# Weight blocks of odd and even depth placed 128 bytes apart, the other way round in the low parts, in a decoder layer on one core

## The chip, the cores and the metric

The program runs on one core of a Trainium2 chip. The metric is the device time of one execution in microseconds (us), as the median of several runs of the same program. Times of single instructions are given in nanoseconds (ns).

## What is computed

One decoder layer over 16 learned and 1024 given tokens of width 1024, all in float32: a gated feed-forward block, a mixing block (stick-breaking attention beside RWKV-7 time mixing), a second gated feed-forward block, and a final norm. Nearly all the arithmetic is in the dense products with the weights:

```
h = h + 0.5 * swiglu(rms_norm(h), ffn1_w_gate, ffn1_w_up, ffn1_w_down)   # 1024 -> 2816 -> 1024
proj = rms_norm(h) @ w_in                                               # 1024 -> 3232 columns
h = h + concat(sb_out, rw_out) @ w_out                                  # 1024 -> 1024
h = h + 0.5 * swiglu(rms_norm(h), ffn2_w_gate, ffn2_w_up, ffn2_w_down)
out = rms_norm(h, final_norm)
```

## The kernel before, in words

**The dense products.** Each float32 operand is split into a high part and a low part in a reduced float32 format, and each product is made of three matmuls (`mm3`): high weights with high activations, high weights with low activations, low weights with high activations. Such a group of three is called a triple here. Every matmul loads its own 128x128 weight block into TensorE while the matmul before it streams its activations past the array; the activations are called the moving operand, 512 columns of it, or 256 to 272, per matmul. A product over a depth of 1024 runs through eight depth blocks k = 0 to 7, so 24 matmuls into one PSUM bank; a product of the down projection runs through the two or four activation tiles of a part.

**The weight tiles.** `loads` fetches a raw weight tile of 128x1024 by DMA; `splits` and `wsplit` turn it into a high tile `whi` (ScalarE copies it) and a low tile `wlo` (VectorE subtracts), two buffers of each, taken in turn (`wtiles`). A tile holds `nk` depth blocks of `nm` columns, one behind the other, so that a depth block starts 512 bytes (for nm = 128) or a multiple of that behind the one before. Each tile is 1056 columns long, 4224 bytes, which is 128 more than 4096, so that the second buffer starts 128 bytes off the first, counted modulo 256. In the built program `whi` starts at byte 26912 and 31136 of each partition, `wlo` at 35360 and 39584: modulo 256 that is 32 and 160, 32 and 160.

**The moving operands.** The normed activations `nh` and `nl` are eight rows of 544 columns, 2176 bytes, so that row k+1 starts 128 bytes off row k modulo 256 (byte 96 for even k, 224 for odd). The activations of the down projection, `ah` and `al`, lie in four buffers of the same 544 columns and alternate in the same way. The normed activations of the second half in the last block, `n2B`, have rows of 512 columns: they keep their place modulo 256 from row to row.

**Places.** The place of a matmul is said here as the start of its moving operand minus the start of a weight block, modulo 256 bytes. It is 64 or 192 throughout these products. In the kernel before the weight blocks of one tile all start at the same byte modulo 256 while the rows of the activations alternate, so that both parts have place 64 for one k, both have 192 for the next, and so on; the other buffer has it the other way round. With `n2B` the place is the same for all k of a tile.

**The order.** A planner in the kernel (class `Clock`) plays the engines against each other with modelled costs and writes out the order of instructions for each engine; TensorE's stream is the dense products (task `dense`), into which triples and short runs of the mixing block's small matmuls are put. The stages the change tells apart are: 0 the first feed-forward block for the first half of the tokens, with its projections; 1 the same block for the second half, its projections and `w_out`; 2 the second feed-forward block for the first half and `w_out` for the second; 3 the second feed-forward block for the second half. Stage 3 and stage 0 make some of their gate and up products by another scheme (`pair`, `quad`) with weight tiles `qh` and `ql` of their own, which the change does not touch.

Of the kernel before, what the change touches and what calls it, by code (L numbers as in the profile page):

```python
# [16 lines left out]
P = 128  # L17
D = 1024
KT = D // P
# [21 lines left out]
WOUT = ((0, 1, 2, 3, 4, 5, 6, 7, 2, 3, 4, 5), (0, 1, 2, 3, 4, 5, 6, 7))  # L41
QF = dict(ffn1=6, ffn2=4)
LINE = 16
NQ, NCC = 6, 6
ROW = 544
AHEAD = 0.1
# [432 lines left out]
class Ker:  # L479
    def __init__(self, tc, A, out):  # L480
        self.tc, self.A, self.out = tc, A, out
        self.clock, self.fast = Clock(), None
        self.wq, self.wr, self.cur, self.flags = [], [], (), {}
        self.nc = NC(tc.nc, self.clock)
        self.need = self.clock.need
        self.after = lambda *aps: self.clock.need(*aps, slack=False)
# [38 lines left out]
        self.clock.ahead = False  # L525
        return raw

    def wtiles(self, nk, nm, pool):

        o = LINE * (pool is self.wx)  # L530
        t = [pool.tile([P, 8 * P + 2 * LINE], F32R, tag=t, bufs=2, name=n) for t, n in (("wh", "whi"), ("wl", "wlo"))]
        return [x[:, o:o + nk * nm].rearrange("p (k c) -> p k c", c=nm) for x in t]

    def wsplit(self, raw, nk, nm, pool):
        self.clock.ahead = True
        self.nsplit = getattr(self, "nsplit", 0) + 1
        hi, lo = self.wtiles(nk, nm, pool)

        self.split(hi, lo, raw, self.nc.gpsimd if self.nsplit < 3 else None)
        self.clock.ahead = False  # L540
        return hi, lo

    def loads(self, plan):

        for x in plan:
            if not isinstance(x, tuple):
                yield x
                continue
            raws = []
            if isinstance(x[0], tuple):  # L550
                for src, ring in zip(x[0], ((self.wp, "wr", 2), (self.fast.q, "wr2", 2))):
                    yield self.need(bank=ring)
                    raws.append(self.wraw(src, *x[1:3], ring))
                    self.hold(raws[-1:])
            else:
                yield self.need(bank=(self.wp, "wr", 2))
                raws.append(self.wraw(*x[:3]))
                self.hold(raws)
            self.wr.append((x, raws))
        self.wr.append(None)  # L560

    def splits(self):

        while True:
            yield lambda: self.wr
            if self.wr[0] is None:
                return
            x, raws = self.wr[0]
            if len(raws) == 2:
                self.wq.append((x, []))  # L570
                yield from self.pair(raws, self.wq[-1][1])
                self.drop(raws)
                self.wr.pop(0)
                continue
            raw, = raws
            pool = self.wx if len(x) > 3 else self.wp
            for tag in ("wh", "wl"):
                yield self.need(bank=(pool, tag, 2))
            self.wq.append((x, self.wsplit(raw, *x[1:3], pool)))
            self.hold(self.wq[-1][1])  # L580
            self.drop((raw,))
            self.wr.pop(0)
# [321 lines left out]
    def ffn(self, nm, h, n, chunks, edge, bank, first=None, hook=None, wx=False, poll=None, resid=None, done=None, wy=False, fast=False, once=False):  # L904
# [22 lines left out]
        def mm(wh, wl, name, c0, c1):  # L927
            yield self.need(*[x[k][:, c0:c1] for k in range(4) for x in n[0:2]], bank=self.nextbank)
            ps = bank(name)[:, :c1 - c0]
            for k in range(KT):  # L930
                if k == 4:
                    yield self.need(*[x[k][:, c0:c1] for k in range(4, KT) for x in n[0:2]])
                self.mm3(ps, wh[:, k, :], wl[:, k, :], nh[k][:, c0:c1], nl[k][:, c0:c1], k == 0, k == KT - 1)
                yield
            return ps

# [48 lines left out]
        def down(dh, dl, part, m, c0, c1):  # L985
            f0, f1 = part
            nf, mw, acts = f1 - f0, KT // (f1 - f0), act[f0:f1]
            yield self.need(acts[0][0][:, c0:c1], acts[0][1][:, c0:c1], bank=self.nextbank)
            pd = bank("pd")[:, :c1 - c0]
            ms = slice((m % mw) * P, (m % mw) * P + P)  # L990
            for j, (ah, al) in enumerate(acts):
                if j:
                    yield self.need(ah[:, c0:c1], al[:, c0:c1])
                self.mm3(pd, dh[:, j, ms], dl[:, j, ms], ah[:, c0:c1], al[:, c0:c1], j == 0, j == nf - 1)
# [218 lines left out]
    def proj(self, items, g, before=None, after=None):  # L1213


        nh, nl = self.n[0:2]
        ranges = ((0, 256), (256, 528)) if g == 0 else ((0, 256), (256, 512)) if len(items) > 1 else ((0, 512),)

        def load(col0, ncol):
            return self.wget(self.wcols("w_in")[:, :, col0:col0 + ncol], KT, ncol)  # L1220
        for i, (c0, c1) in enumerate(ranges):
            if before:
                yield from before(i)
            for col0, ncol, evac in items:
                if i == 0 or len(items) > 1:
                    wh, wl = yield from load(col0, ncol)
                yield self.need(*[x[k][:, c0:c1] for k in range(KT) for x in (nh, nl)], bank=self.nextbank)
                ps = self.bank("pd")[0:ncol, :c1 - c0]
                for k in range(KT):
                    self.mm3(ps, wh[:, k, :], wl[:, k, :], nh[k][:, c0:c1], nl[k][:, c0:c1], k == 0, k == KT - 1)  # L1230
# [52 lines left out]
    def plan(self):  # L1283
# [13 lines left out]
        def ffn(nm, poll=False, wx=False, fast=False, once=False):  # L1297
# [41 lines left out]
        yield from ffn("ffn1", wx=True, fast=True)  # L1339
        yield from proj(0)  # L1340
        yield from ffn("ffn1", once=True)
        yield from proj(1)
        yield from wout(False)
        yield from ffn("ffn2", True)
        if "woutat" not in F:
            yield lambda: F.get("f2b")
            F["woutat"] = None
            yield from wout(False)
        yield from ffn("ffn2", wx=True, fast=True)

    def projections(self, g, before, after):

# [667 lines left out]
    def wout(self, h2, n, hook, ready=None, late=False):  # L2020
# [5 lines left out]
        def one(m, wh, wl, i):  # L2026
# [3 lines left out]
            yield self.need(*[x[k][:, cs] for k in range(KT) for x in n[0:2]], bank=self.nextbank)  # L2030
            pd = self.bank("pwo")[:, 0:256]
            for k in range(KT):
                self.mm3(pd, wh[:, k, :], wl[:, k, :], n[0][k][:, cs], n[1][k][:, cs], k == 0, k == KT - 1)
                yield
            hd = h2[:, m, cs]
            with self.urgent():
# [504 lines left out]
```

## Time and profile before

| | |
|---|---|
| median of 3 runs | 2247.16 us (2245.82 to 2251.48) |
| profiled execution, its own time | 2247.88 us |
| its span, first to last instruction | 2246.0 us |
| TensorE matmul busy | 2218.6 us, 99% of the span |
| weight loads busy (beside the matmuls) | 1967.9 us, 88% |
| VectorE, ScalarE, GpSimd busy | 69%, 49%, 26% |
| granted TensorE clock, mean | 0.997 of full speed |

The recorded duration of a matmul reaches beyond the start of the next one, since matmuls are pipelined and their ends are modelled. What a matmul costs in a dense stretch is the step from its start to the next start; the differences in duration between neighbouring matmuls follow the differences in those steps.

### The profile page before, as it was taken

The page shows a single profiled execution, that of the slowest core. Times are in us where ns is not written, and L with a number is a line of the kernel's source. Part 1 is how long each engine was busy: PE and PEld are TensorE (multiplying, and loading weights), DVE is VectorE, ACT ScalarE, POOL GpSimd, SP SyncE. Part 2 cuts the span into 40 slices and gives each one's busy share as a digit, 9 for nine tenths or more (in the row PEclk, how much of TensorE's full clock was granted, in tenths as well). Part 3 has the DMA queues.
Part 4 walks back from the last instruction along what each step waited for, and adds up shares of the span by engine and source line. Part 5 has one row for each costly group of instructions (what it writes and reads, how often), then busy time and mean ns, then how long its engine had stood idle before and what let it go on. Part 6 is the DMA issues. An engine that isn't in the chain of part 4 may idle for free.

```text
span 2246.0 us, 41718 instructions
## 1 busy us (share of the span) xinstructions
PE 2218.6 (99%) x16409; PEld 1967.9 (88%) x16409; DVE 1547.6 (69%) x2633; ACT 1096.6 (49%) x2176; POOL 574.1 (26%) x722
## 2 busy tenths in 40 slices
PE   9999999999999999999999999999999999999998
PEld 8999999999878888778888988887878899899998
DVE  5887776476666655566576787556777656897774
ACT  5444444534444434655435564445656436455444
POOL 1321111013143231542012325314443101322120
PEclk9999999999999999999999999999999999999999
DMA  5543232545643232332556534334222433333332
GB/s 171 179 113 104 85 104 79 167 129 144 198 112 99 74 100 91 100 93 76 158 142 190 164 101 118 86 93 118 79 83 61 132 118 120 116 104 106 110 89 82
DMA packets 408730, 257.61 MB, mean 115 GB/s; under 512 B 45005, under 2 KB 392357, under 8 KB 408534
## 3 DMA queue, kind: packets, MB, share of 16 engines
q1 hardware_dynamic: 408534, 254.95, 39.3%
q8 instruction: 129, 2.11, 0.4%
q14 instruction: 67, 0.55, 0.1%
HBM read 220.90 MB, written 33.99 MB: 113 GB/s over the span
## 4 chain that ended last, share of the span: by engine, by line
PE 91%; DVE 3%; issue 2%; ACT 2%; DMA 1%; SPq 1%; POOL 0%; DVEq 0%; ACTq 0%; POOLq 0%
PE pd L107 33%; PE pu L107 21%; PE pg L107 21%; PE pwo L107 3%; PE px L107 3%; PE po L107 2%; PE pz L107 2%; PE pat L107 2%; DVE wlo L107 1%; SPq L107 1%; PE pG L107 1%; ACT whi L107 1%; PE psw L107 0%; PE pp L107 0%; DVE nl L107 0%
## 5 line engine op out<-in xcount | busy, mean ns | idle before, releaser
L107 ACT ACTIVATE whi<-wraw 128x1024 fp32r<-128x1024 f32 x314 | 330.7, 1053 | 324.7 <-PE pd L107 195.8
L107 DVE TENSOR_TENSOR wlo<-wraw,whi 128x1024 fp32r<-128x1024 f32 (+1 forms) x312 | 406.8, 1306 | 99.4 <-ACT whi L107 91.4
L107 PE MATMUL pd<-ah,whi 128*128 128x512 f32 (+2 forms) x944 | 323.8, 343 | 2.9 <-DVE h L107 2.0
L107 PE MATMUL pd<-ah,wlo 128*128 128x512 f32 (+2 forms) x944 | 319.3, 338 | 1.2 <-DVE wlo L107 1.2
L107 PE MATMUL pd<-al,whi 128*128 128x512 f32 (+2 forms) x944 | 317.8, 337 | 0.6 <-DVE al L107 0.3
L107 PE MATMUL pd<-nh,whi 128*128 128x256 f32 (+7 forms) x648 | 209.5, 323 | 0.0
L107 PE MATMUL pu<-nh,whi 128*128 128x512 f32 (+3 forms) x576 | 205.6, 357 | 0.0
L107 PE MATMUL pd<-nh,wlo 128*128 128x256 f32 (+7 forms) x648 | 204.3, 315 | 0.0
L107 PE MATMUL pd<-nl,whi 128*128 128x256 f32 (+7 forms) x648 | 203.4, 314 | 0.0
L107 PEld LDWEIGHTS pd<-ah,whi 128*128 128x128 f32 x944 | 177.5, 188 | 24.9 <-DVE h L107 3.4
L107 PE MATMUL pu<-nh,wlo 128*128 128x512 f32 (+3 forms) x576 | 197.9, 344 | 0.0
L107 POOL TENSOR_TENSOR qs<-wraw 128x512 f32<-128x512 f32 x64 | 106.1, 1660 | 358.1 <-DVE ql L107 133.5
L107 PE MATMUL pg<-nh,whi 128*128 128x512 f32 (+3 forms) x536 | 196.9, 367 | 0.8 <-ACT nh L107 0.6
L107 PE MATMUL pu<-nl,whi 128*128 128x512 f32 (+3 forms) x576 | 196.8, 342 | 0.0
L107 PEld LDWEIGHTS pd<-ah,wlo 128*128 128x128 f32 x944 | 177.5, 188 | 21.2 <-DVE wlo L107 2.1
L107 PEld LDWEIGHTS pd<-al,whi 128*128 128x128 f32 x944 | 177.6, 188 | 19.3 <-DVE al L107 2.0
L107 PE MATMUL pg<-nh,wlo 128*128 128x512 f32 (+3 forms) x536 | 188.7, 352 | 0.1
L107 PE MATMUL pg<-nl,whi 128*128 128x512 f32 (+3 forms) x536 | 187.6, 350 | 0.9 <-DVE nl L107 0.9
L107 DVE SCALAR_TENSOR_TENSOR h<-pd,h 128x256 f32<-128x256 f32 (+1 forms) x200 | 107.5, 541 | 76.7 <-PE pd L107 76.2
L107 POOL TENSOR_TENSOR al<-sl,ah 128x512 fp32r<-128x512 f32 (+2 forms) x45 | 73.5, 1632 | 317.7 <-ACT ah L107 314.6
L107 PEld LDWEIGHTS pd<-nh,whi 128*128 128x128 f32 (+2 forms) x648 | 120.1, 185 | 11.8 <-issue 3.1
L107 PEld LDWEIGHTS pd<-nh,wlo 128*128 128x128 f32 (+2 forms) x648 | 119.8, 185 | 8.4 <-DVE wlo L107 0.2
(395 smaller groups left out, 5633.3 us busy)
## 6 DMA issues: line engine op xcount, KB each, us to landing
wraw<-in_ffn_w_gate_dram SPq DMA_DIRECT2D x90, 512.0 KB
wraw<-in_ffn_w_up_dram SPq DMA_DIRECT2D x90, 512.0 KB
wraw<-in_ffn_w_down_dram SPq DMA_DIRECT2D x88, 512.0 KB
wraw<-in_w_in_dram SPq DMA_DIRECT2D x54, 512.0 KB
wraw<-in_w_out_dram SPq DMA_DIRECT2D x20, 512.0 KB
s<-rkvd SPq DMA_DIRECT2D x18, 256.0 KB
raw<-qkvd SPq DMA_DIRECT2D x16, 264.0 KB
raw<-qkvd SPq DMA_DIRECT2D x16, 256.0 KB
```

Source lines behind the costliest of these rows:

```text
L107: self._c.trace(self._n, op, lambda: f(*a, **k), out, [x for x in args if isinstance(x, bass.AP)], k)
```

## The change

The table `LAY` names, by stage and by kind of weight (gate, up and projection columns under "up"; "down"; "w_out"), the tiles that get a new layout; all entries are the same, `W3`. In such a tile the depth blocks of one parity lie in the first half, those of the other parity in the second half, and the second half starts 32 columns, 128 bytes, later than half the tile. Which parity lies later is set by the entry, by the part (the two pairs of `W3` differ in it) and by the buffer's turn, which flips with each tile taken from the pool. With row k of the activations 128 bytes off row k-1, this gives in the built program: the high part has place 192 for every k and in both buffers, the low part has place 64. That holds for 1240 of the triples with 512 columns; in 32 it is the other way round (high 64, low 192). With `n2B` the place now alternates with k, high and low against each other. In all 4945 matmuls read weights from another byte than before.

A tile with the new layout has four dimensions, and `row` picks a depth block from either kind. 201 high tiles are written by ScalarE and 201 low tiles by VectorE in that pattern, with the raw tile viewed in the same order. The rest passes the layout along: `laid` sets it while the plan is read, `loads` keeps it beside the raw tile, `splits` hands it to `wsplit`. Apart from the shapes of these writes the order of instructions on every engine is the same as before, buffers lie at the same bytes, and no instruction is added or removed.

```diff
+W3 = ((1, 1), (1, 0))
+LAY = {(1, "up"): W3, (1, "down"): W3, (2, "up"): W3, (2, "down"): W3, (2, "w_out"): W3, (3, "up"): W3, (3, "down"): W3}
...
-    def wtiles(self, nk, nm, pool):
-        o = LINE * (pool is self.wx)
+    def wtiles(self, nk, nm, pool, lay=None):
+        wx = pool is self.wx
+        pool.turn = getattr(pool, "turn", 1) ^ 1
         t = [pool.tile([P, 8 * P + 2 * LINE], F32R, tag=t, bufs=2, name=n) for t, n in (("wh", "whi"), ("wl", "wlo"))]
-        return [x[:, o:o + nk * nm].rearrange("p (k c) -> p k c", c=nm) for x in t]
+        r = []
+        for x, l in zip(t, lay or (None, None)):
+            if l is None or wx or nm % P:
+                o = LINE * wx
+            else:
+                split, odd = l
+                odd ^= pool.turn
+                h = nk * nm // 2 + 2 * LINE
+                if split:
+                    r.append(bass.AP(x.tensor, x.offset + h * odd, [x.ap[0], [nm, nk // 2], [h * (1 - 2 * odd), 2], [1, nm]]))
+                    continue
+                o = 2 * LINE * odd
+            r.append(x[:, o:o + nk * nm].rearrange("p (k c) -> p k c", c=nm))
+        return r
+
+    @staticmethod
+    def row(w, k):
+        return w[:, k // 2, k % 2] if len(w.shape) > 3 else w[:, k]
...
+        if len(hi.shape) > 3:
+            raw = raw.rearrange("p (a b) c -> p a b c", b=2)
...
-                self.mm3(ps, wh[:, k, :], wl[:, k, :], nh[k][:, c0:c1], nl[k][:, c0:c1], k == 0, k == KT - 1)
+                self.mm3(ps, self.row(wh, k), self.row(wl, k), nh[k][:, c0:c1], nl[k][:, c0:c1], k == 0, k == KT - 1)
...
+        def laid(gen, stage):
+            for x in gen:
+                if isinstance(x, tuple):
+                    src = x[0][0] if isinstance(x[0], tuple) else x[0]
+                    self.lay = LAY.get((stage, next((n for n in ("down", "w_out") if n in src.name), "up")))
+                yield x
```

## Rows read from the trace of the kernel before

**Rows 1.** The page: span, busy time by engine, granted clock in 40 slices.

```profile
span 2246.0 us, 41718 instructions
PE 2218.6 (99%) x16409; PEld 1967.9 (88%) x16409; DVE 1547.6 (69%) x2633; ACT 1096.6 (49%) x2176; POOL 574.1 (26%) x722
...
PEclk9999999999999999999999999999999999999999
```

**Rows 2.** The page: chain of work that ended last, by engine.

```profile
PE 91%; DVE 3%; issue 2%; ACT 2%; DMA 1%; SPq 1%; POOL 0%; DVEq 0%; ACTq 0%; POOLq 0%
```

**Rows 3.** Waits of TensorE for weight tiles: us in total, times, longest.

```profile
PE pwo L107 <- DVE wlo L107: 1.4, 2, 0.8
PE pd L107 <- DVE wlo L107: 1.2, 2, 0.8
```

**Rows 4.** Groups by shape, TensorE, first of each triple: count, busy us, mean ns, idle.

```profile
L107 PE MATMUL pd<-ah,whi 128*128 128x512 f32 x464 | 187.0, 403 | 0.9 <-DVE h L107 0.5 <-ACT ah L107 0.3
...
L107 PE MATMUL pg<-nh,whi 128*128 128x512 f32 x328 | 135.6, 413 | 0.1
...
L107 PE MATMUL pu<-nh,whi 128*128 128x512 f32 x312 | 129.8, 416 | 0.0
...
L107 PE MATMUL pd<-nh,whi 128*128 128x512 f32 x168 | 67.2, 400 | 0.0
```

**Rows 5.** Busy time in 1080:1126, projections: us, PE (x), PEld, DVE, clock, DMA.

```profile
1080.00:1126.00 46.00, 46.00 (x202) 36.51 (x201) 5.52 (x8) 1.00 0.64 189
```

**Rows 6.** Groups by shape in 1090.49:1091.00: one triple, both parts at place 64.

```profile
L107 PE MATMUL pd<-nh,wlo 128*128 128x512 f32 x1 | 0.4, 394 | 0.0
L107 PE MATMUL pd<-nl,whi 128*128 128x512 f32 x1 | 0.4, 392 | 0.0
L107 PE MATMUL pd<-nh,whi 128*128 128x512 f32 x1 | 0.4, 390 | 0.0
```

**Rows 7.** The next triple, 1091.18:1091.69: both parts at place 192.

```profile
L107 PE MATMUL pd<-nh,wlo 128*128 128x512 f32 x1 | 0.4, 398 | 0.0
L107 PE MATMUL pd<-nh,whi 128*128 128x512 f32 x1 | 0.4, 392 | 0.0
L107 PE MATMUL pd<-nl,whi 128*128 128x512 f32 x1 | 0.4, 388 | 0.0
```

**Rows 8.** Groups in 812.91:813.42 (operand `ah`): place 192, next triple at 192 too.

```profile
L107 PE MATMUL pd<-ah,whi 128*128 128x512 f32 x1 | 0.4, 392 | 0.0
L107 PE MATMUL pd<-al,whi 128*128 128x512 f32 x1 | 0.4, 388 | 0.0
L107 PE MATMUL pd<-ah,wlo 128*128 128x512 f32 x1 | 0.4, 392 | 0.0
```

**Rows 9.** Groups in 819.12:819.63: place 64, the triple before at place 64 too.

```profile
L107 PE MATMUL pg<-nh,wlo 128*128 128x512 f32 x1 | 0.4, 398 | 0.0
L107 PE MATMUL pg<-nl,whi 128*128 128x512 f32 x1 | 0.4, 391 | 0.0
L107 PE MATMUL pg<-nh,whi 128*128 128x512 f32 x1 | 0.4, 388 | 0.0
```

**Rows 10.** Timeline, first and last of 22 matmuls, operand n2B, place 64 throughout.

```profile
1934.17 0.40 PE L107 MATMUL pg<-n2Bh,wlo 128*128 128x512 f32 x1
...
1939.07 0.40 PE L107 MATMUL pg<-n2Bh,wlo 128*128 128x512 f32 x1
```

**Rows 11.** Groups of 256 columns: whole program, and 1962.65:1963.75 (tiles qh, t4h).

```profile
L107 PE MATMUL pd<-ah,whi 128*128 128x256 f32 x304 | 86.2, 284 | 2.0 <-DVE h L107 1.5 <-DVE h2B L107 0.5
...
L107 PE MATMUL pwo<-n2Bh,whi 128*128 128x256 f32 x128 | 35.6, 278 | 0.0
...
L107 PE MATMUL pg<-t4h,qh 128*128 128x256 f32 x4 | 1.1, 276 | 0.0
```

**Rows 12.** Groups by shape, VectorE: low weight tiles; output in four pieces; output in one.

```profile
L107 DVE TENSOR_TENSOR wlo<-wraw,whi 128x1024 fp32r<-128x1024 f32 x308 | 403.1, 1311 | 99.3 <-ACT whi L107 91.4 <-DMA wraw<-in_w_in_dram 2.4 <-DMA lod<-st 1.7
...
L107 DVE TENSOR_TENSOR nl<-pxn,nh 128x512 fp32r<-128x512 f32 x8 | 5.1, 685 | 2.8 <-ACT nh L107 2.8
...
L107 DVE TENSOR_TENSOR atl<-pat,ath 128x512 fp32r<-128x512 f32 x48 | 30.8, 683 | 16.3 <-ACT ath L107 16.1
```

More of the change, by code (lines that the diff above doesn't have):

```diff
@@ L483, in __init__ @@
         self.wq, self.wr, self.cur, self.flags = [], [], (), {}
+        self.lay = None
         self.nc = NC(tc.nc, self.clock)
@@ L526, in wraw, with wsplit @@
         return raw
-    def wtiles(self, nk, nm, pool):
-        o = LINE * (pool is self.wx)
+    def wtiles(self, nk, nm, pool, lay=None):
+        wx = pool is self.wx
+        pool.turn = getattr(pool, "turn", 1) ^ 1
         t = [pool.tile([P, 8 * P + 2 * LINE], F32R, tag=t, bufs=2, name=n) for t, n in (("wh", "whi"), ("wl", "wlo"))]
-        return [x[:, o:o + nk * nm].rearrange("p (k c) -> p k c", c=nm) for x in t]
-    def wsplit(self, raw, nk, nm, pool):
+        r = []
[15 more added lines that the diff above has]
+        return w[:, k // 2, k % 2] if len(w.shape) > 3 else w[:, k]
+    def wsplit(self, raw, nk, nm, pool, lay):
         self.clock.ahead = True
         self.nsplit = getattr(self, "nsplit", 0) + 1
-        hi, lo = self.wtiles(nk, nm, pool)
+        hi, lo = self.wtiles(nk, nm, pool, lay)
+        if len(hi.shape) > 3:
+            raw = raw.rearrange("p (a b) c -> p a b c", b=2)
         self.split(hi, lo, raw, self.nc.gpsimd if self.nsplit < 3 else None)
@@ L548, in loads @@
                 continue
-            raws = []
+            raws, lay = [], self.lay
             if isinstance(x[0], tuple):
@@ L558, in loads @@
                 self.hold(raws)
-            self.wr.append((x, raws))
+            self.wr.append((x, raws, lay))
         self.wr.append(None)
@@ L567, in splits @@
                 return
-            x, raws = self.wr[0]
+            x, raws, lay = self.wr[0]
             if len(raws) == 2:
@@ L578, in splits @@
                 yield self.need(bank=(pool, tag, 2))
-            self.wq.append((x, self.wsplit(raw, *x[1:3], pool)))
+            self.wq.append((x, self.wsplit(raw, *x[1:3], pool, lay)))
             self.hold(self.wq[-1][1])
@@ L993, in down @@
                     yield self.need(ah[:, c0:c1], al[:, c0:c1])
-                self.mm3(pd, dh[:, j, ms], dl[:, j, ms], ah[:, c0:c1], al[:, c0:c1], j == 0, j == nf - 1)
+                self.mm3(pd, self.row(dh, j)[:, ms], self.row(dl, j)[:, ms], ah[:, c0:c1], al[:, c0:c1], j == 0, j == nf - 1)
             hd = h[:, m, c0:c1]
@@ L1229, in proj @@
                 for k in range(KT):
-                    self.mm3(ps, wh[:, k, :], wl[:, k, :], nh[k][:, c0:c1], nl[k][:, c0:c1], k == 0, k == KT - 1)
+                    self.mm3(ps, self.row(wh, k), self.row(wl, k), nh[k][:, c0:c1], nl[k][:, c0:c1], k == 0, k == KT - 1)
                     yield
@@ L1338, in ffn @@
                 yield from [down(*PARTS[-1], q) for q in range(4)]
[L1339 to L1344, printed above, removed]
+        def laid(gen, stage):
[4 more added lines that the diff above has]
+                yield x
+        yield from laid(ffn("ffn1", wx=True, fast=True), 0)
+        yield from laid(proj(0), 0)
+        yield from laid(ffn("ffn1", once=True), 1)
+        yield from laid(proj(1), 1)
+        yield from laid(wout(False), 1)
+        yield from laid(ffn("ffn2", True), 2)
         if "woutat" not in F:
@@ L1347, in plan @@
             F["woutat"] = None
-            yield from wout(False)
-        yield from ffn("ffn2", wx=True, fast=True)
+            yield from laid(wout(False), 2)
+        yield from laid(ffn("ffn2", wx=True, fast=True), 3)
     def projections(self, g, before, after):
@@ L2032, in one @@
             for k in range(KT):
-                self.mm3(pd, wh[:, k, :], wl[:, k, :], n[0][k][:, cs], n[1][k][:, cs], k == 0, k == KT - 1)
+                self.mm3(pd, self.row(wh, k), self.row(wl, k), n[0][k][:, cs], n[1][k][:, cs], k == 0, k == KT - 1)
                 yield
```

## The prediction

> **What bounds the kernel now.** I read the page first: TensorE is busy for 99% of the span, and the granted clock stands at 9 tenths or more (the level of 2.4 GHz) in all 40 slices [rows 1]. The chain of work that ended last is TensorE for 91% [rows 2]. So time goes only if TensorE's own instructions take less, or is added if they take more or have to wait. Waits for weight tiles come to 1.4 and 1.2 us [rows 3]; the other engines have room, VectorE with 31% of its time free.
>
> Which of TensorE's instructions does the change touch? Every triple with 512 columns in the stages named: the first matmuls of the triples count 464, 328, 312 and 168, together 1272 [rows 4]. The means of 400 to 416 ns there hold waits and switches from small matmuls in front of a triple; the cost of the pure stream is read from a stretch without them. Between 1080 and 1126 us, 46.00 us hold 202 records, of which two reach over the edges: 200 steps of 230 ns [rows 5]. Two neighbouring triples of that stretch have durations of 390, 392, 394 [rows 6] and 392, 388, 398 [rows 7], mean 392.3. So a duration is about 162 ns longer than the step, and I work with differences of durations.
>
> Now the point of the whole case. Those two triples are alike in every respect but one: in the first, the weights of both parts lie at place 64, in the second at place 192. The three roles (high-high, high-low, low-high, in order of time) change by +2, -4 and +4 ns. A fixed role and a fixed shape thus give different times at different places, and the pattern comes back with every second k through the stretch. That two placements give different times is what the change can work on. The sums are 1176 and 1178, mean 1177, which is 691 ns for a triple after taking off three times 162.
>
> **What the Trainium skill says against it.** First the row: the same role takes 388 or 392, 394 or 398 ns by place alone [rows 6, 7]. The page "TensorE: Matmul & The Clock Gate" of the Trainium skill (Part 2, step 1) says that loading the next weights takes no read bandwidth from the running matmul, since each has its own port. By that, bytes could not matter and the change would be worth 0 us. The trace does not agree with it that far; the rule comes back as a rival.
>
> **The change, part by part.**
>
> *Matmuls with 512 columns.* After the change the high part has place 192 and the low part 64 for nearly all k. I take the roles one by one.
> - High-high at 192, the next weights the same block: the row exists, 392 [rows 7]. Half of these triples stood at 390 [rows 6], so the mean rises by 1.
> - High-low, own weights at 192, the weights loaded during it at 64. No row has this role so. Its bounds are 388 and 392 as it is at the two uniform places [rows 6, 7]. A step of the same kind, own weights at 192 and the next at 64 against the operand that streams, stands at the end of a group, in the third role: there it takes 392 instead of the 398 of a uniform 192 and the 394 of a uniform 64 [rows 8, 7, 6]. That speaks for the low bound or near it: I take 389, against a mean of 390 now: -1.
> - Low-high, own weights and next weights both at 64: 394 as in [rows 6], against a mean of 396 now: -2.
>
> By roles the sum is 1175 instead of 1177, -2. There is a second reading. In the trace the dear step is the one that is third in a row at the same place (394, 398), and the cheap ones come just after the place has changed (390, 388 in [rows 6, 9]; 392 in [rows 8]). A triple of the new kind has the weights that are loaded during it at 192, 64, 64 (each against the operand that streams meanwhile) and so never three in a row: 392 for the change to 192, 390 for the change to 64, 392 for the second at 64 is 1174, less by 3; with the 388 of [rows 9] for the change to 64, less by 5. I take -3 ns for a triple, 1272 x 3 = 3.8 us.
>
> The bounds: below, three steps at the least duration seen, 388 [rows 7]: 1164, -13 ns, -16.5 us. Above, the steps where a place is kept for a long time: 22 matmuls with 21 steps from 1934.17 to 1939.07 us are 233.3 ns each [rows 10], 3.3 more than the 230 of [rows 5], +10 ns a triple, +12.7 us. I come back to this number as a rival.
>
> *Matmuls with 256 columns.* Some 270 triples on rows that alternate change one of their parts, and some 200 on `n2B`. The rows stand at 284 with alternating rows (with a few waits in it), 278 with `n2B`, and 276 in a product of the other scheme, where high and low have different places [rows 11]. Best case: 470 triples go to 276, which is 270 x 3 x -8 and 200 x 3 x -2, -7.7 us; worst: those of `n2B` go from 278 to 284, 200 x 3 x 6, +3.6 us. Which places help at 256 columns no row tells, and the change flips one part of a triple only; I take -0.3 us, near nothing.
>
> *Writing the tiles.* 201 copies and 201 subtractions write in eight pieces (or two, or four) instead of one. A subtraction whose output lies in four pieces, each in its own row, takes 685 ns, one with its output in one piece 683 [rows 12]: 2 ns for three jumps, some 5 for seven. On a subtraction of 1311 ns that is 201 x 5 = 1.0 us of VectorE in all, which hides in its 31% of free time. If the cover failed, it would be felt where TensorE waits for a tile, which it did 4 times [rows 3]: 0.02 us. I cost it at nothing. Transfers, their order and their sizes stay.
>
> **The sum**: -3.8 - 0.3 = -4.1 us. The profiled execution took 2247.88 us, so 2243.8; the median of the runs lies 0.7 lower than it, so I forecast **2243 us**. Anything within 0.3% (6.7 us, 2240.4 to 2253.9) is about what a measurement of this kernel cannot tell from no change.
>
> **The rivals.**
>
> *Every step near its best.* If what makes a step dear is only the run of equal places, breaking the run in every triple may also relieve the first and third roles. For it: one triple with a change inside comes to 392 + 388 + 392 = 1172 already [rows 8]; and products with differing places at 256 columns stand at the least seen, 276 [rows 11]. Against it: those products have an operand that keeps its place, and after the change the third role still has 64 next to 64. With -5 to -13 ns it gives -6.4 to -16.5 us, middle -10: **2237 us**.
>
> *The kept place is what costs (slower).* With the same place for operand and weights throughout, a step takes 233.3 ns [rows 10], against 230.0 where the place flips from triple to triple [rows 5]: +10 ns a triple. After the change each role keeps its own place for every k, 192 for the high part and 64 for the low one. If steps depend on a matmul's own place being the same as in the triple before, and not on the weights loaded meanwhile, the change takes away just the flips that kept the cost down: 1272 x 10 = 12.7 us, **2260 us** as the median; at half, since high and low still differ, 2253.5. It decides against the kernel from 6.7 us / 1272 = 5.3 ns a triple on. Against it: two neighbouring triples with the same place, as at the end and the start of groups, are not dear: 392 + 388 + 392 = 1172 and 388 + 391 + 398 = 1177 [rows 8, 9].
>
> *Nothing changes.* By the rule of the skill's page above, or because gains and losses by role cancel: +1 for the first role, -2 for the third and +1 for the second, inside its bounds, are 0, **2247 us** as the median. For it: the two uniform places differ by 2 ns in 1177 although single roles differ by 4, so what one step saves the next pays back.
>
> *The change does not do what it says.* It would then be the layout that is off, say if the turn of a buffer fell out of step with its pool. The bytes in the built program exclude it: 1240 of 1272 triples stand as described, the other 32 reversed.
>
> **How the numbers follow.** Small gain as forecast: 0.38, 2240 to 2246. Nothing changes: 0.13. Every step near its best: 0.36, 2231 to 2241. The kept place: 0.13, 2252 to 2260. Faster by over 0.3% is the third case, all but its weak end, and the strong end of the first: 0.37. Slower by over 0.3% is the last but for its weak end: 0.11. The same is left with 0.52. The range takes in, downwards, the larger part of the third case, to 2233; upwards, nothing changes with some loss at 256 columns and the weak end of the last, to 2253. What it leaves out is some 0.07 below and 0.11 above.
>
> **What would show it.** In a stretch of projections without breaks like [rows 5], 46 us should hold 201 steps instead of 200; all triples should look alike, for even and odd k, with about 392, 388 to 390, 392 to 394 ns. The weight loads, the waits for tiles and the clock should stay. If the three durations come to 1171 or less, the case of every step near its best holds; at 1182 or more, the kept place. If triples at 512 columns fall and the time does not, a wait for `wlo` has grown, or the 256-column products lost it. The forecast is wrong if the second role does not come down to 390 or below.

## The result and the profile after

The changed kernel takes 2241.0 us as the median of 11 runs (2239.62 to 2242.41), the kernel before 2247.16 us as the median of 11 (2244.46 to 2251.48): 6.2 us less, ratio 0.9973, 95% interval 0.9963 to 0.9982. A second measurement of the same two programs gave 2240.18 against 2246.55 us, ratio 0.9973 (0.9961 to 0.9984). The forecast was 2243 us in a range from 2233 to 2253.

The page of the profiled execution after, its span, busy times, clock and chain of waits:

```profile
span 2237.6 us, 41718 instructions
PE 2210.1 (99%) x16409; PEld 1964.8 (88%) x16409; DVE 1553.4 (69%) x2633; ACT 1097.1 (49%) x2176; POOL 571.3 (26%) x722
PEclk9999999999999999999999999999999999999999
PE 95%; DVE 3%; ACT 1%; issue 1%; DMA 0%; POOL 0%; DVEq 0%; ACTq 0%; POOLq 0%
```

Beside [rows 1, 2] nothing has moved to another engine: TensorE is as full as before, at the same clock to a tenth, and the chain still runs through it. The span is 8.4 us shorter (2246.0 before); why that is more than the 6.2 of the medians is told below.

The unbroken stretch of projections, which answers to [rows 5], and two neighbouring triples in it, which answer to [rows 6, 7] (groups by shape in 1090.84:1091.35, where k is of one parity; in the triple ahead of it, 1090.15:1090.66, the rows are the same but for a second `wlo` at the window's edge):

```profile
1079.00:1125.00 46.00, 46.00 (x203) 36.81 (x202) 20.62 (x24) 18.80 (x37) 0.00 (x0) 1.00 0.65 191
```

```profile
L109 PE MATMUL pd<-nh,wlo 128*128 128x512 f32 x1 | 0.4, 392 | 0.0
L109 PE MATMUL pd<-nh,whi 128*128 128x512 f32 x1 | 0.4, 391 | 0.0
L109 PE MATMUL pd<-nl,whi 128*128 128x512 f32 x1 | 0.4, 388 | 0.0
```

46 us now hold 203 records instead of 202, so 201 steps instead of 200, and each triple is 391 + 388 + 392 = 1171 ns, with no difference between even and odd k. Before it was 1176 and 1178 by turns. From start to start, over the 57 unbroken triples of this stretch, a step takes 227.8 ns after and 229.9 ns before.

In the whole program the groups of second and third roles fall and the first stays; here those of `ah`, which stood at 403 [rows 4], 396 and 392 before, in the order of the lines:

```profile
L109 PE MATMUL pd<-ah,whi 128*128 128x512 f32 x464 | 187.0, 403 | 1.9 <-DVE h L109 1.6 <-ACT ah L109 0.3
L109 PE MATMUL pd<-ah,wlo 128*128 128x512 f32 x464 | 182.8, 394 | 1.3 <-DVE wlo L109 1.3
L109 PE MATMUL pd<-al,whi 128*128 128x512 f32 x464 | 181.2, 390 | 0.4 <-DVE al L109 0.3
```

TensorE's waits for weight tiles stay as in [rows 3], 1.4 and 1.3 us against 1.4 and 1.2 (us in total, times, longest):

```profile
PE pwo L109 <- DVE wlo L109: 1.4, 2, 0.8
PE pd L109 <- DVE wlo L109: 1.3, 2, 0.8
```

**Where the time came from.** Since both programs give TensorE the same matmuls in the same order, the two traces can be laid on each other matmul by matmul, and a triple's time is taken from its first start to the start of the next. Over the triples that have no pause or change of shape in them in either trace (the rows of 256 columns also hold triples of the other scheme, which the change does not touch):

| triples | count | change after minus before, us | second profile of the change |
|---|---|---|---|
| 512 columns | 1005 | -4.0 | -3.9 |
| 256 columns, operand `n2B` | 438 | -1.4 | -1.4 |
| 256 columns, others | 1067 | -0.4 | -0.4 |
| 264 and 272 columns (not touched) | 878 | +0.1 | +0.05 |

That is -5.8 us, and the second profile repeats each row to 0.1 us. The rest of the span's 8.4 us lies mostly in the stage change near 1303 us: some 1.7 us less lost at the lower clock and a pause of 1.9 instead of 2.7 us (the last experiment).

### The profile page after: what moved, and what is told of

The parts are those of the page before. It is cut to its first block, busy times and chain, and to the rows that moved or that the text cites. A ratio compares the mean times of both kernels' runs of the same rounds, so it can differ in the third digit from the quotient of the medians.

```text
span 2237.6 us, 41718 instructions
## 1 busy us (share of the span) xinstructions
PE 2210.1 (99%) x16409; PEld 1964.8 (88%) x16409; DVE 1553.4 (69%) x2633; ACT 1097.1 (49%) x2176; POOL 571.3 (26%) x722
## 4 chain that ended last, share of the span: by engine, by line
PE 95%; DVE 3%; ACT 1%; issue 1%; DMA 0%; POOL 0%; DVEq 0%; ACTq 0%; POOLq 0%
PE pd L109 34%; PE pu L109 22%; PE pg L109 21%; PE pwo L109 4%; PE px L109 3%; PE po L109 2%; PE pz L109 2%; PE pat L109 2%; DVE wlo L109 1%; PE pG L109 1%; PE psw L109 0%; PE pp L109 0%; ACT whi L109 0%; DVE nl L109 0%; PE pss L109 0%
## 5 line engine op out<-in xcount | busy, mean ns | idle before, releaser
L109 DVE TENSOR_TENSOR wlo<-wraw,whi 128x1024 fp32r<-128x1024 f32 (+1 forms) x312 | 413.6, 1328 | 99.2 <-ACT whi L109 95.5
L109 POOL TENSOR_TENSOR qs<-wraw 128x512 f32<-128x512 f32 x64 | 100.4, 1571 | 362.8 <-DVE ql L109 139.9
```

The lines of the kernel that those rows point to most:

```text
L109: self._c.trace(self._n, op, lambda: f(*a, **k), out, [x for x in args if isinstance(x, bass.AP)], k)
```

## The experiments

### A bare stream of matmuls

The kernel has nothing but matmuls: groups of 24 with 512 columns or 48 with 256, each with its own pattern of places, one behind the other; the decoder layer is left out. The core of it, shortened (`hi`, `lo`: the places; 0 means that the place flips with the operand, as before; `row` is 128 where the operand of odd k lies 128 bytes later, 0 where it keeps its place; `xh`, `xl`, `wh`, `wl` are the byte positions of the high and low operand and weights, `xl` a multiple of 256 behind `xh`; `W` is the number of columns):

```python
xh = 1024 + row * (k % 2)
wh = (k % 2) * 512 + ((xh - hi) % 256 if hi else 64)
wl = 1792 + (k % 2) * 512 + ((xh - lo) % 256 if lo else 64)
s += [(wh, xh, W), (wh, xl, W), (wl, xh, W)]
```

> A kernel of nothing but matmuls, float32r, in groups of 24 (512 columns) or 48 (256 columns), each group with its own place or pattern of places; the rest of the program is left out. Theory 1 (a step is dear when the place of the weights is the same three times in a row, whichever place it is): the pattern of the change (high 192, low 64, operand flipping) and its reverse (high 64, low 192) both come to about 228 ns a step, the pattern of before to 230, and a place kept for 24 matmuls to 233 at every one of the 16 places. Theory 2 (it depends on which place the weights in use have and which the weights loaded meanwhile, so on the order of the two places): the change 228, the reverse 231 to 232, before 230, and the kept place not the same at all 16 places. If nothing depends on place in this bare stream, all groups stand at one value and the difference in the kernel comes from its other traffic.

Groups by shape of this kernel (mean duration in ns; `odd` the operand flips, `keep` it keeps its place; then high and low place: `h` 192, `s` 64, `alt` flipping; `one`: a single operand and two weight blocks at place 0 (`a`) and 192 (`m`)):

```profile
L28 PE MATMUL w_odd_alt_alt<-xs,ws 128*128 128x512 f32 x24 | 5.7, 393 | 0.0
L28 PE MATMUL w_odd_h_s<-xs,ws 128*128 128x512 f32 x24 | 5.6, 391 | 0.0
L28 PE MATMUL w_odd_s_h<-xs,ws 128*128 128x512 f32 x24 | 5.7, 394 | 0.0
L28 PE MATMUL w_odd_h_alt<-xs,ws 128*128 128x512 f32 x24 | 5.6, 390 | 0.0
L28 PE MATMUL w_odd_h_h<-xs,ws 128*128 128x512 f32 x24 | 5.6, 390 | 0.0
L28 PE MATMUL w_odd_alt_s<-xs,ws 128*128 128x512 f32 x24 | 5.7, 392 | 0.0
L28 PE MATMUL w_odd_alt_h<-xs,ws 128*128 128x512 f32 x24 | 5.7, 393 | 0.0
L28 PE MATMUL one_a<-xs,ws 128*128 128x512 f32 x24 | 5.6, 389 | 0.0
L28 PE MATMUL one_m<-xs,ws 128*128 128x512 f32 x24 | 5.8, 395 | 0.0
```

As steps from start to start, without the first six of a group: before 229.9 ns, the change 227.7, its reverse 232.4, high part alone 227.7, both parts at 192 227.7, low part alone 229.7. No other engine works here, so the difference comes from TensorE's own stream, and the bare stream repeats the program's 229.9 and 227.8. Theory 1 falls on the reverse and on the kept places, which do not all stand at 233; theory 2 stands: what matters most is that the high part is at 192 and not at 64. With the high part at 192 the place of the low part makes no difference (227.7 three times). Elsewhere it does: a low part at 192 gives 231.2 instead of 229.9 where the high part flips, and 232.4 instead of 230.9 (low part at 64 too) where the high part is at 64. A single operand whose weights all stay at place 0 steps at 226.7, less than the change; at 192 it steps at 233.5, at 64 at 229.1, and the most is 234.5, at 160.

### High part alone, low part alone, the reverse

Each is the changed kernel with another layout in one line (the first two also give the part that isn't shifted the same four-dimensional view):

```diff
-W3 = ((1, 1), (1, 0))
+W3 = ((1, 1), None)      # high alone
+W3 = (None, (1, 0))      # low alone
+W3 = ((1, 0), (1, 1))    # reverse
```

High alone: 

> Only the high parts follow the operand (place 192 throughout), the low parts lie as before. Theory 1 (three times the same loaded place in a row is what costs): the loads stand at 192, then 64 or 192, then 64, never three alike, so the gain of the change stays, 2241 us. Theory 2 (what counts is the place of the high part, in use at 192 while the next one is loaded at 64): by the bare stream the pattern steps at 227.71 ns, the change at 227.71, before at 229.88, so the whole gain stays, 2241 us, and the low part of the change is idle. If the two parts share the gain, 2244.

Low alone: 

> Only the low parts follow the operand (place 64 throughout), the high parts lie as before. Theory 1: loaded places 64, 64, 192 or 192, 64, 64 by turns, never three alike within a triple, so 2241 to 2243 us. Theory 2: 229.71 ns a step in the bare stream against 229.88, 3816 steps x 0.17 = 0.6 us, so 2246.5, as before. If the two parts share the gain, 2244.

Reverse: 

> The reverse of the change: high parts at place 64, low parts at 192, throughout. Theory 1: the loads stand at 64, 192, 192, never three alike, a gain as by the change, 2241 to 2243 us. Theory 2: 232.35 ns a step in the bare stream against 229.88 before, 3816 x 2.5 = 9.4 us at most; the change gave three quarters of what the bare stream says (6.2 of 3816 x 2.17 = 8.3 us), so 7 us slower than before, 2254.

| kernel | us | before, us | ratio (95%) | 512-column triples, us | 256-column triples, us | step in the 57 triples, ns |
|---|---|---|---|---|---|---|
| high alone | 2242.2 | 2247.27 | 0.9975 (0.9966 to 0.9984) | -4.2 | -0.9 | 227.8 |
| low alone | 2244.96 | 2247.27 | 0.9990 (0.9981 to 0.9998) | +0.2 | -1.1 | 229.9 |
| low alone, again | 2246.34 | 2246.55 | 0.9995 (0.9985 to 1.0004) | +0.2 | -1.1 | 229.9 |
| reverse | 2250.04 | 2247.27 | 1.0015 (1.0007 to 1.0024) | +5.6 | -0.5 | 232.2 |

The columns of triples are those without a pause, against the first profile of before, as above; the last column is the unbroken stretch, 229.9 before and 227.8 in the change. Now the triples themselves, groups by shape in the same stretch. High alone reads as the change, 391, 388 and 392 ns, in the triples with the low part at 64 and in those with it at 192. Low alone, low part at 64 in both, high part first at 192 (1091.35:1091.84), then at 64 (1092.03:1092.54):

```profile
L109 PE MATMUL pd<-nh,wlo 128*128 128x512 f32 x1 | 0.4, 398 | 0.0
L109 PE MATMUL pd<-nh,whi 128*128 128x512 f32 x1 | 0.4, 392 | 0.0
L109 PE MATMUL pd<-nl,whi 128*128 128x512 f32 x1 | 0.4, 388 | 0.0
...
L109 PE MATMUL pd<-nh,wlo 128*128 128x512 f32 x1 | 0.4, 394 | 0.0
L109 PE MATMUL pd<-nl,whi 128*128 128x512 f32 x1 | 0.4, 392 | 0.0
L109 PE MATMUL pd<-nh,whi 128*128 128x512 f32 x1 | 0.4, 390 | 0.0
```

The reverse, two triples in a row (1099.79:1100.30 and 1100.49:1101.00):

```profile
L109 PE MATMUL pd<-nl,whi 128*128 128x512 f32 x1 | 0.4, 398 | 0.0
L109 PE MATMUL pd<-nh,wlo 128*128 128x512 f32 x1 | 0.4, 393 | 0.0
L109 PE MATMUL pd<-nh,whi 128*128 128x512 f32 x1 | 0.4, 390 | 0.0
...
L109 PE MATMUL pd<-nh,wlo 128*128 128x512 f32 x1 | 0.4, 398 | 0.0
L109 PE MATMUL pd<-nl,whi 128*128 128x512 f32 x1 | 0.4, 394 | 0.0
L109 PE MATMUL pd<-nh,whi 128*128 128x512 f32 x1 | 0.4, 391 | 0.0
```

The low part alone leaves the triples as in [rows 6, 7], although each low block now lies at 64: even the low-high role, whose own weights are the moved ones, stays at 394 and 398. So that role's time doesn't come from its own weights. It goes with the high blocks before and behind it. The high block of the next k is loaded during the low-high matmul; seen from the operand that streams meanwhile, it stands at 64 in the change and at 192 in the triple with 398. But it stands at 64 in the triple with 394 as well; what differs there from the change is the triple's own high block, at 64 instead of 192. Over the whole program, in runs of 512-column triples, the step of this role is:

| own high block, next high block | kernel | triples | step, ns |
|---|---|---|---|
| 192, 64 | change | 785 | 229.9 |
| 64, 64 | before | 364 | 232.3 |
| 64, 192 | reverse | 785 | 233.8 |
| 192, 192 | before | 364 | 235.4 |

With the high part alone and with the low part alone the place of the low block shows no effect. In the reverse it has: the high-low role there, with the high block at 64 and the low block loaded during it at 192, steps at 233.8 ns, against 229.6 in before with both at 64. And the triples of the reverse differ by turns (1181 and 1183 above, 1186 for the third) although every k has the same places, so a step depends on more than the blocks at hand. Theory 1 (three alike in a row) expected 2241 to 2243 us of the reverse and is out. Of the low part alone its expectation counted wrongly: seen from the streaming operand the loads there stand at 64, 64, 64 and 192, 64, 192 by turns, so three alike do occur; but the dearest role, 398, comes in the triple that has no three alike, which speaks against the theory as well. Theory 2 expected 2254 of the reverse, more than the 2250 that came.

### Writing in pieces, without the shift

```diff
-                h = nk * nm // 2 + 2 * LINE
+                h = nk * nm // 2
```

> The odd blocks lie behind the even ones as in the change, written in the same two, four or eight pieces, but without the 128 bytes between, so every place is as before. What is left of the change is the writing. Theory 2 (place alone): 2247 us as before. Rival (writing in pieces, or the other timing of the tiles, gives the 2 us by which the low half and the reverse beat their streams): 2245. If pieces cost VectorE or ScalarE time that is felt, 2248 or more.

2246.6 us against 2247.05, ratio 0.9998 (0.9989 to 1.0007): the writing costs nothing and gives nothing that can be told from noise (the 512-column triples stay within 0.02 us, those of 256 columns off `n2B` come to -0.2 us). On VectorE it is visible. The low weight tiles, here and in the change:

```profile
L109 DVE TENSOR_TENSOR wlo<-wraw,whi 128x1024 fp32r<-128x1024 f32 x308 | 406.1, 1321 | 99.0 <-ACT whi L109 95.7 <-DMA lod<-st 1.7 <-PE pat L109 0.3
```

```profile
L109 DVE TENSOR_TENSOR wlo<-wraw,whi 128x1024 fp32r<-128x1024 f32 x308 | 409.9, 1333 | 99.1 <-ACT whi L109 95.5 <-DMA lod<-st 1.7 <-PE pat L109 0.3
```

From 1311 ns in [rows 12] to 1321 with pieces and 1333 with pieces and the gap, 6.8 us of VectorE in all instead of the 1.0 that the prediction put down, and none of it reaches TensorE.

### More places in the bare stream

The same kind of kernel with both parts at each of sixteen places behind a flipping operand (`w_follow`, `v_follow` with 256 columns, `a` is place 0, each letter 16 bytes more), some with parts at differing places, and steps of 4 bytes about place 0 with a kept operand (`near`, `below`); the decoder layer is left out again.

> Bare stream again, the rest of the program left out: groups of 24 matmuls with 512 columns, 48 with 256, at more places. If only the difference of the two addresses within 256 bytes counts, a weight block 256 bytes further on (far_a, far_m) and both operands moved together by 64 bytes (move_a, move_m) step as in the first such kernel: 226.7 ns at place 0, 233.5 at place 192. With an operand that flips and both parts following it (w_follow), place 192 gives 227.7 ns as there; if a place near 0 is good for an operand that flips too, some place of the sixteen stands at 226.7 and beats the change by 1 ns a step, 3816 steps, 3.8 us; if not, 192 is the least and the change has what there is to have. The low part makes no difference with the high part at 192 (w_high): 227.7. At 256 columns (v_follow) the least is 113.3 if a flipping operand can reach what a kept one has, 115.5 or more if not.

```profile
L28 PE MATMUL w_follow_m<-xs,ws 128*128 128x512 f32 x24 | 5.7, 394 | 0.0
L28 PE MATMUL w_follow_a<-xs,ws 128*128 128x512 f32 x24 | 5.7, 392 | 0.0
L28 PE MATMUL near_a<-xs,ws 128*128 128x512 f32 x24 | 5.7, 391 | 0.0
L28 PE MATMUL w_high_a<-xs,ws 128*128 128x512 f32 x24 | 5.7, 392 | 0.0
L28 PE MATMUL w_high_i<-xs,ws 128*128 128x512 f32 x24 | 5.7, 394 | 0.0
```

In these groups only the difference within 256 bytes counts: a weight block 256 bytes further on steps at 226.7 and 233.5 as before, operand and weights moved together by 64 bytes at 227.9 (while still settling, 226.7 at the end) and 233.5. But misses stand beside it. The high part at 192 with the low part at 0 (`w_high_a`) or 128 (`w_high_i`) steps at 229.9 and 232.9 and not at the 227.7 expected. `w_follow_m` has, byte for byte, the addresses of the group `w_odd_h_h` of the first such kernel, which stepped at 227.7; here it steps at 232.2, behind another group. The addresses of place 16 with a kept operand gave 226.7 there (`one_b`) and 228.2 here (`near_e`). And `near_a`, place 0 again, takes steps of 234, 231, 233, 236, 224, 231, 236, 228, 232 and 231 ns before it falls into 226, 227, 227. So the stream seems to have a memory: places allow a rhythm, and what ran before decides whether, and how soon, it is reached. The two kernels ran once each, on two chips, so these pairs alone do not show that the group before is the cause; but the ten steps of `near_a` are one execution, and in one profile of the kernel before whole groups of `n2B` with 256 columns, one place throughout, stand at 340 ns a triple and others at 353. No place behind a flipping operand beat the 227.7 of the change; the least here was 229.9, at place 0. Since 192 itself came to 232.2 here, this does not show that none would. With 256 columns and a flipping operand the least was 116.7 (115.5 in the first such kernel), so the 113.3 of a kept one was not reached. Steps below the change were seen with a kept operand alone, 226.7 at places 0, 4 and 16.

### A version with place 0

Rows of 2304 bytes would keep every operand at its place. They need 1 to 2 kB more in each partition than the second attention stage leaves free, so one buffer of that stage had to go, and a control has that change alone:

```diff
-        dict(raw=1, qs=4, kh=4, vs=2, sg=8, f=2, at=4, z=2, t=2, o=1)]
+        dict(raw=1, qs=4, kh=4, vs=2, sg=7, f=2, at=4, z=2, t=2, o=1)]
```

> The change with one buffer less in the second attention stage (8 to 7 of the tag sg), a control for the two kernels below, which need its room. With nothing lost 2241 us; a wait in the attention stage for the missing buffer would give 2243 or more.

On top of it, for the operands `n`, shortened (`NROW` is the length of their rows in columns; the other kernel does the same to the tiles of `ah` and `al` and their products `down`; both have gaps ahead of the operand, so that the place comes to 0):

```diff
-LAY = {(1, "up"): W3, ...
+KEEP = ((0, 1), (0, 1))
+LAY = {(1, "up"): KEEP, ...
+NROW, AROW = 576, 544
-        half = [[self.hp.tile([P, 4, ROW], ...
+        half = [[self.hp.tile([P, 4, NROW], ...
+        self.hp.tile([P, LINE], F32, name="gap")
```

Operands `n`: 

> On top of that control: rows of the operands n are 2304 bytes apart instead of 2176, so they keep their place for every k, and the weights of all their 512-column products stand at place 0, high and low, every k. Theory 2 with the bare stream (place 0 kept: 226.65 ns a step; 256 columns kept: 113.3 at any place): by the rows of the change, 512 columns 510 triples x 5.5 = 2.8 us, 256 columns 473 x 12 = 5.7 us, and if 264 and 272 columns go as 256 (to 349 and 360 a triple) 150 x 14 + 274 x 15.5 = 6.3 us: 12 to 15 us under the control, 2226 to 2229. Rival (the fast rhythm at place 0 is reached only in a long unbroken stream, since one group of the bare stream took ten steps to fall into it): at 512 columns 229 or more, no gain or a loss there, 2230 to 2236.

Operands `ah` and `al`: 

> On top of that control: the rows of the operands ah and al are 2304 bytes apart, so they keep their place, and the weights of their 512-column products stand at place 0 throughout; the products of n stay as in the change. Theory 2: 512 columns 356 triples x 6.5 = 2.3 us, 256 columns 223 x 11.8 = 2.6 us, 272 columns 144 x 15 = 2.2 us, 7 us under the control, 2234. Rival as for the kernel before: 2236 to 2239.

The control takes 2292.67 us (ratio 1.0204, 1.0190 to 1.0218), the two versions 2292.74 and 2292.18, where 12 to 15 us and 7 us less than the control were expected. The planner writes another order around the missing buffer, and TensorE waits in the control (time in us, times, longest):

```profile
PE pwo L111 <- ACT n2Bh L111: 11.7, 2, 10.1
PE pg L111 <- ACT t1h L111: 10.8, 3, 7.2
PE pwo L111 <- DVE wlo L111: 8.0, 6, 5.2
```

So the price of the room is some 52 us against the change (2241.0), and neither version can be had this way. Part of it is the clock: over the control's runs the mean granted clock is 0.989, against 0.997 in the change, which by itself makes some 18 us (an estimate, 0.008 of 2290 us). Their places can still be read against the control, though each has an order of its own. Operands `n` at place 0, in the unbroken stretch (1094.66:1095.17), and first roles with 256 columns (`pd`), then those of the control:

```profile
L111 PE MATMUL pd<-nh,whi 128*128 128x512 f32 x1 | 0.4, 389 | 0.0
L111 PE MATMUL pd<-nl,whi 128*128 128x512 f32 x1 | 0.4, 389 | 0.0
L111 PE MATMUL pd<-nh,wlo 128*128 128x512 f32 x1 | 0.4, 389 | 0.0
...
L111 PE MATMUL pd<-nh,whi 128*128 128x256 f32 x240 | 70.3, 293 | 0.0
```

```profile
L111 PE MATMUL pd<-nh,whi 128*128 128x256 f32 x240 | 69.7, 291 | 0.0
```

At 512 columns the triple does come to 3 x 389 = 1167 ns, 4 less than in the change. Over the 589 triples of `n` without a pause it is 684.9 ns from start to start against 686.1 in the control, 0.7 us in all: 352 of them stand at 680, most of the others at more. At 256 columns the version loses what it won: 357.9 against 352.1 ns a triple, 510 x 5.8 = 3.0 us. Of these triples 322 stand at place 0 (358.8 ns) and 189 at place 128 (356.5 ns). With `ah` and `al` it is 685.8 against 687.1, and 357.1 against 351.7. The 113.3 ns a step that the bare stream showed for a kept operand with 256 columns were for places 64 and 192; places 0 and 128 had not been tried there, and they are the wrong ones. So there is no version here that beats the change.

### The same kernels once more

By its triples the low part alone gains 0.9 us, yet its first measurement said 2.3. Its profile differs from that of before near 1303 us, where the stages change. There TensorE pauses before the product `pp`, for 2.7 us in before and 1.9 to 2.3 us in the other profiles, a wait put down to nothing that the profile shows (waits of TensorE in before, 1290:1330):

```profile
PE pp L107 <- issue: 2.7, 1, 2.7
```

Then, in most of them, the granted clock stands for some time at 0.50, the lower of its two levels (1.2 instead of 2.4 GHz). Three programs were run again for a second profile.

> The kernel before once more, for a second profile. After a pause of 2.7 us near 1303 us its first profile shows TensorE at half clock for some 7 us, which costs 3.4 us; the change's first profile shows 1.7 us lost there, the one with the low parts alone none. Theory 3 (this loss belongs to a kernel, by the time at which it comes to the pause): the second profile shows 3.4 us again, time 2247 us, ratio 1.000. Rival (it is drawn anew in every execution): the second profile shows another value, 0 or 1.7 us, and the three kernels do not keep their order.

> The changed kernel once more. Theory 3: 1.7 us lost at half clock near 1300 us again, time 2241 us. Rival: another value, 0 or 3.4 us. Either way the triples with 512 columns step as in the first profile, 227.9 ns in long stretches, since nothing but addresses sets them.

> The low parts alone once more, whose 512-column steps were as before (+0.2 us in all) while its time was 2.3 us less. Theory 3: no loss at half clock near 1300 us again, time 2245 us, so the 2 us are the clock's. Rival: a loss of 1.7 or 3.4 us this time; the time then is nearer to 2246 or 2247, and the first 2.3 us were a draw.

Busy time by stretch, granted clock in the third column from the right. Before, first and second profile:

```profile
1305.00:1310.00 5.00, 5.00 (x85) 4.96 (x76) 4.29 (x5) 2.88 (x8) 3.23 (x3) 0.53 0.48 136
1310.00:1315.00 5.00, 5.00 (x62) 4.73 (x61) 2.65 (x5) 2.23 (x4) 1.73 (x2) 0.79 0.28 80
```

```profile
1305.00:1310.00 5.00, 2.87 (x102) 2.86 (x103) 4.19 (x7) 4.72 (x12) 1.60 (x2) 0.69 0.30 77
1310.00:1315.00 5.00, 5.00 (x56) 4.83 (x54) 3.10 (x6) 0.85 (x3) 4.13 (x5) 0.62 0.67 196
```

The change, first and second:

```profile
1300.00:1305.00 5.00, 4.15 (x109) 4.14 (x110) 4.24 (x8) 4.09 (x12) 2.12 (x2) 0.67 0.29 80
```

```profile
1300.00:1305.00 5.00, 4.19 (x109) 4.18 (x110) 4.14 (x7) 4.05 (x12) 2.17 (x2) 0.66 0.33 98
```

The low part alone, first and second:

```profile
1305.00:1310.00 5.00, 5.00 (x70) 4.82 (x69) 4.69 (x6) 2.38 (x8) 4.83 (x5) 1.00 0.73 210
```

```profile
1305.00:1310.00 5.00, 3.81 (x107) 3.80 (x108) 4.28 (x7) 4.43 (x12) 1.93 (x3) 0.64 0.32 87
1310.00:1315.00 5.00, 5.00 (x57) 4.83 (x57) 3.25 (x6) 1.13 (x3) 3.18 (x4) 0.68 0.50 147
```

A stretch of 5 us at clock c loses about 5 x (1 - c), an estimate: before 3.4 us both times, the change 1.7 both times, the low part alone 0 and then 1.8 + 1.6 = 3.4. So the loss isn't the kernel's own, and theory 3 falls with the third program; its median went the same way, from 2244.96 to 2246.34 us. Before against itself came to 2248.0 against 2246.55, ratio 1.0005 (0.9996 to 1.0014), which shows how far two measurements of one program lie apart. Whether before and the change draw from the same values is not settled by two profiles each, but every run lists its mean granted clock. Compared at the same clock (mean time in us, number of runs):

| granted clock | before | change | low alone, first and again |
|---|---|---|---|
| 0.997 | 2246.3 (19) | 2241.5 (11) | 2247.0 (3), 2245.3 (2) |
| 0.998 | 2245.6 (20) | 2239.4 (6) | 2244.8 (5), 2243.9 (4) |

So the gain of the change, 4.8 to 6.2 us at equal clock, is not the clock's. The low part alone lies within 2 us of before; its first runs had a mean clock of 0.9980, the second 0.9969, which is the way its time went.

## Why the prediction was right, and where its reasons were not

- **What bounds the kernel, and the stretch.** As said: TensorE's own steps, 201 of them in 46 us, triples alike for even and odd k, waits, loads and clock as they were.
- **The high-high role** was put at 392 ns, 1 more than before, and is 391; over the program its step rose by 0.3.
- **The high-low role** was put at 389, and is 388. Over the program its step fell by 2.8 ns for the triples that stood at 64 and by less than 0.1 for the others, 1.4 on average where 1 was forecast.
- **The low-high role** was put at 394, and is 392. Here the step failed in its reason: "own weights and next weights both at 64: 394 as in [rows 6]". The runs show that its own weights do not matter (394 and 398 by turns with the low part at 64 throughout), and that the next high block alone does not set it either: with own and next weights at 64 as in [rows 6] it takes 392, because the triple's high block is at 192 (a step of 229.9 ns against 232.3). It fell by 2.1 ns for the triples that stood at 64 and 3.8 for the others, 3.0 on average, where 2 was forecast.
- **The sum for a triple** was -3 ns, and the triples without a pause show -4.0 on average, -4.0 us in all against -3.8. In the unbroken stretch it is -6. That is the bound that the prediction set for its rival of every step near its best (1171 or less), and in long streams that rival holds. Over the program a third of it is lost, much of it at the end of a group: the last triple of a group gained 2.3 ns, the others 4.7. The triples that already had a high block at 192 ahead of one at 64, as in [rows 8], gained 0.5, and the last triples ahead of another shape 0.2. The prediction priced the stretch at too little and took it for all triples, two errors that nearly cancel; that the total came out close is luck to that extent.
- **The second reading**, three of the same place in a row, gave the right number for a wrong cause. The reverse never has three alike, and its triples are slower by 5.6 us; the low part alone shows the dear 398 without three alike.
- **Nothing changes.** Loads that take no bandwidth from the running matmul, as the Trainium skill has it ("TensorE: Matmul & The Clock Gate", Part 2, step 1), would make the bare stream's groups equal. With one operand and nothing but the place of the weights changed they step at 226.7 to 234.5 ns, so the rule, read that way, does not agree with this case. Whether it is read bandwidth that is lost, no run shows.
- **The kept place** as the slower rival lost its price: after the change each part keeps its place, and the steps are the least measured with a flipping operand. Its 233.3 [rows 10] belonged to an operand that keeps its place as well.
- **256 columns** was the mis-sized term: -0.3 us forecast, -1.8 measured. Nearly all is `n2B`, 438 triples for -1.4 us; the 203 of them whose places changed went from 346.3 to 340.5 ns, -1.2 us, the 276 ns a matmul that the prediction had named as the best case but had not counted on. The others, -0.4, were as near to nothing as said, and writing in pieces without the shift shows -0.2 of it too.
- **Writing the tiles** took more of VectorE than worked out (6.8 us, not 1.0), and nothing of the end, as said.
- **The end.** -4.0 - 1.8 = -5.8 us from the matmuls, against -4.1; the medians say -6.2 and -6.4. The remaining half microsecond is within what before shows against itself.

## What to carry to other kernels

Where a stream of matmuls is at its limit, lay two neighbouring products of the same shape side by side in the trace: a difference of a few ns between them that comes back with every second one may have its cause in addresses, and addresses can be chosen where there is room. Try one part at a time, as well as the reverse, before the explanation is believed; here half of the change did nothing for the 512-column products, and the reverse made them 5.6 us slower where the change made them 4.0 us faster. And read a stretch where the clock can drop in more than one profile before a difference of 2 us is given to a change.

## What was not expected of the hardware

- The time of a 512-column matmul depends on where the weight blocks lie against the operand that streams, counted modulo 256 bytes: from 226.7 to 234.5 ns a step in a stream where nothing else runs.
- The same addresses gave 227.7 and 232.2 ns a step behind different predecessors in two kernels, and a stream at place 0 took ten steps to settle at 226.7. Why the places matter, and why the place 0 that is best at 512 columns is a bad one at 256 (119.6 ns a step for a kept operand in the program, against 113.3 at 64 and 192 in the bare stream), was not found out.
- After pauses of 1.9 to 2.7 us the granted clock stood at 0.50 for stretches that cost 1.7 or 3.4 us, or did not drop at all, in executions of the same program.
